# Hybrid block on one core: first modulations as plain fp32 on four column groups, filter steps in the opening stage

## The chip, the core and the metric

The kernel runs on one core of a Trainium2 chip. A core has TensorE (PE, the matmul array, with its weight loads listed apart as PEld), VectorE (DVE), ScalarE (ACT), GpSimd (POOL) and SyncE (SP). Each engine takes its instructions strictly in the order in which the built program lists them, and waits on semaphores where one needs another's result. Weights come from device memory by DMAs that SP issues; POOL and ACT issue some smaller ones. The metric is the device time of one execution in microseconds (us); lower is better.

## What is computed

One layer of a diffusion block over 256 latent tokens `x` and 256 context tokens `ctx`, width 2048. Only the start concerns the change:

```
mod   = silu(c)     @ w_ada + b_ada        # 6 x 2048 numbers for x
mod_c = silu(c_ctx) @ w_ada[:, :4096] + b_ada[:4096]   # shift and scale for ctx
u     = x   * (1 + scale)   + shift        # first two parts of mod
u_ctx = ctx * (1 + scale_c) + shift_c
parts = u @ w_in                            # keys, values, gates, Hyena, ...

# Hyena filters: independent of x, from three small weight matrices
hid = sin(sin(feats @ w1 + b1) @ w2 + b2)
h   = (hid @ w3) * window                   # 256 x (2 orders, 2 directions, 1024)
kf  = fft(h_fwd, h_bwd)                     # spectra, used later by the long convolutions
```

So the first 4096 columns of `w_ada` (2048 x 4096 in fp32, 33.5 MB) must be read and multiplied by two vectors before any projection of `u` can start.

## The kernel before

**Splitting.** The large products run in a reduced type called fp32r. To keep fp32 accuracy each operand is split into a high and a low part: `split` (line 136) copies the high part on ACT (line 138) and subtracts it on DVE (line 139), and a product becomes three: high by high, high by low, low by high (`cm_block`, line 215, lines 220, 221, 223).

**First modulations.** The loop at line 381 goes over four quarters `q` of 512 columns, and over `part` (0 shift, 1 scale). For each it reads 2048 x 512 of `w_ada` in four DMAs of 1 MB into a page `raw` (`load4`, line 319), splits half a page at a time (`split_ring`, line 324: high part to `ring`, low part to a `wlo` buffer), and accumulates 32 products of 512 columns into the bank `pmod` (lines 396 and 397). Their stationary operand `csw` (line 205) has 128 columns: high of c, high of c_ctx, low of c, low of c_ctx, repeated 32 times; only four rows of `pmod` are used. `mod_columns` (line 369) turns the four rows into columns with four small products by `sel` (line 374).

**Beside it.** A list `later` holds steps of the quarter before: `mod_columns`, four `modulated` (line 357: transpose 128 columns of x and ctx, scale and shift on ACT, split), two `keys` (line 346: 48 products each of 256 columns into four banks) and one `gates_in` (line 337: 24 such products). One is taken after every second half page. Two calls of `next(filt)` run the two small sine layers of the Hyena filters (`filters`, line 241) here.

**The filter steps.** The eight large steps of `filters` (line 271 on: for four groups of 256 channels by two orders) each load a window and two slices of `w3` (POOL's DMAs), make four plain fp32 products (line 281), multiply by the window, add and subtract the two directions (lines 282, 289, 290), split (line 292), and take 30 fp32r products of 256 columns with the Fourier matrix (`dft_mm`, lines 237 to 239). They use three pages each. Before, they are emitted in pairs after each of the four blocks of the DeltaNet's value projection (lines 685 to 698), where 192 products of 256 columns stand ready on PE per block.

**Order and buffers.** A scheduler orders each engine's list from the program's order and a timeline of its own. There are seven pages of 8 KB per partition (`k8`); in this stage they hold x and ctx (`xt`), `raw`, `csw`, and in filter steps `dfts`, `win`, `smdf`, `shl`. Accumulators of this stage come from four banks called `ps`, of which `gates_in` keeps one.

Of the kernel before, what the change touches and what calls it, by code (L numbers as in the profile page):

```python
# [16 lines left out]
P = 128  # L17
# [63 lines left out]
def tile_block(ctx: ExitStack, tc: tile.TileContext, A: dict, out: bass.AP):  # L81
# [6 lines left out]
    # SBUF slots by size in KB per partition: projections' operands 16, one more 16, pages 8, small ones  # L88
# [20 lines left out]
    def page(name, *shapes, dt=F32):  # L109
        """One 8 KB slot, cut into tiles of the given free shapes."""  # L110
        return cut(slot([P, 2048], "k8", name, dt), shapes)
# [21 lines left out]
    def bc(ap, shape):  # L133
        return ap.to_broadcast(shape)

    def split(src, hi, lo):
        """src = hi + lo exactly, each of at most 12 significant bits"""
        copy(out=hi, in_=src)  # L138
        tt_(out=lo, in0=src, in1=hi.bitcast(F32), op=SUB)  # L139
# [9 lines left out]
    # work that goes on beside the projections: some steps of it with each tile of weights  # L149
# [42 lines left out]
    def as_rows(ap):  # L192
# [9 lines left out]
    # stationary for one k-tile: columns hi of c, hi of c_ctx, lo of c, lo of c_ctx, over and over  # L202
    cs4 = slot([P, KT, 4], "k1", "cs4", F32R)
    split(csil.rearrange("p a k -> p k a"), cs4[:, :, 0:2], cs4[:, :, 2:4])
    csw = page("csw", (KT, P), dt=F32R)
    nc.vector.tensor_copy(out=csw.rearrange("p k (r c) -> p k r c", c=4),
                          in_=bc(cs4.bitcast(F32).unsqueeze(2), [P, KT, 32, 4]))
    sel = cst.tile([4, 2], F32, name="sel")
    tt_(out=sel, in0=ident[0:4, 0:2], in1=ident[0:4, 2:4], op=ADD)
# [5 lines left out]
    def cm_block(ps, wh, wl, ch, k, acts, first, last):  # L215
        """channel-major: 128 columns of w stationary; acts: (column range of the bank, hi, lo) of 256 tokens"""
# [98 lines left out]
    ring = slot([P, 4, 1024], "m16", "ring", F32R)  # L315
    turn = [0]
    raws = {}

    def load4(ap, k0, c0):
        raw = page("raw", (4, 512))  # L320
        nc.sync.dma_start(out=raw, in_=ap[k0 * P:(k0 + 4) * P, c0:c0 + 512].rearrange("(k p) c -> p k c", p=P))
        return raw

    def split_ring(raw):
        """two k-tiles by 512 columns, in two parts, with more of them under way"""
        n = turn[0]
        turn[0] += 1
        hi = ring[:, n % 4].rearrange("p (k c) -> p k c", k=2)
        lo = slot([P, 2, 512], ("whi", "wlo")[n % 2], "wlo", F32R)
        split(raw, hi, lo)  # L330
        return hi, lo

    psk = [mm_ps() for _ in range(4)]      # projected keys of the DeltaNet, by 128 channels

    pga = sc_ps()                          # and the inputs of its gates

    def gates_in(k0):
        raw, wh, wl = [slot([P, 4, P], "wraw", "wg", t) for t in (F32, F32R, F32R)]
        nc.sync.dma_start(out=raw, in_=w_in[k0 * P:(k0 + 4) * P, C_AB:C_AB + P].rearrange("(k p) c -> p k c", p=P))
        split(raw, wh, wl)  # L340
# [5 lines left out]
    def keys(k0):  # L346
        if k0 % 4 == 0:
            raws["k"] = load4(w_in, k0, C_DK)
        wh, wl = split_ring(raws["k"][:, k0 % 4:k0 % 4 + 2, :])
# [19 lines left out]
    def mod_columns(mod, part, pmod, q):  # L369
        """four times 128 columns of one modulation, from rows"""  # L370
        row = slot([4, 512], "k2", "modrow")
        copy(out=row, in_=pmod[0:4, :])
# [7 lines left out]
    later = []  # L380
    for q in range(4):
# [6 lines left out]
        for part in range(2):  # L388
            pmod = sc_ps()
            for kb in range(8):  # L390
                if kb % 2 == 0:
                    raw = load4(w_ada, kb * 2, part * D + q * 512)
                wh, wl = split_ring(raw[:, (kb % 2) * 2:(kb % 2) * 2 + 2, :])
                for k in range(2):
                    kt = kb * 2 + k
                    mm(pmod, csw[:, kt, :], wh[:, k, :], start=(kt == 0), stop=False)
                    mm(pmod, csw[:, kt, :], wl[:, k, :], start=False, stop=(kt == KT - 1))
                if later and (part * 8 + kb) % 2 == 1:
                    later.pop(0)()
            later.insert(0, lambda mod=mod, part=part, pmod=pmod, q=q: mod_columns(mod, part, pmod, q))  # L400
# [5 lines left out]
        if q in (1, 2):  # L406
            later.append(lambda: next(filt))
# [3 lines left out]
    # the remaining small vectors  # L411
# [20 lines left out]
    # lower bounds: softmax over the layers (one), cumulated, less the first  # L432
# [14 lines left out]
    def proj_cm_ctx(col0):  # L447
        """256 columns of w_in, channel-major: two banks of 128 channels by x 256 | ctx 256"""
# [11 lines left out]
    def proj_cm(wap, col0, ah, al):  # L460
        """256 columns, channel-major: one bank of 128 channels by 2 chunks by x 256"""
# [10 lines left out]
    def tm_accum(pss, ah, al, wap, k0, nk, c0):  # L472
        """512 columns, token-major: pss[i] += a[tokens of tile i].T w, a in two parts by k-tile"""
# [1067 lines left out]
```

## Time and profile before

| | us |
|---|---|
| median of 3 runs | 2402.77 |
| lowest, highest | 2392.48, 2405.41 |
| profiled execution: span from first to last instruction | 2405.1 |
| opening stage (to the last key and gate product) | 0 to 164.6 |
| value and query projections of the DeltaNet, with the filter steps | 166.3 to 372 |
| TensorE busy over the span | 2303.7 (96%) |

The profiled execution's span of 2405.1 us stands beside 2405.41 us for the slowest of the three runs, so hardly anything lies around the span; the median of the runs is 2.3 us below it. TensorE's busy time counts modelled ends of pipelined matmuls, so the true pace of a matmul is read from the distance between two starts, not from its duration. The granted clock of TensorE has two levels, 2.4 GHz (1.00) and 1.2 GHz (0.50).

### The profile page before, as it was taken

The numbers are of one execution on the slowest core, as the hardware profiler recorded it, in microseconds if no ns is written. First come the engines' busy times: TensorE is split into PE (matmuls) and PEld (weight loads), VectorE is DVE, ScalarE is ACT, GpSimd is POOL, SyncE is SP. The second block draws the span as 40 slices with busy tenths as digits, with TensorE's granted clock in tenths as the row PEclk, the third lists the DMA queues.
The fourth block names the chain that finished last, engine by engine and source line by source line (L and its number), as shares of the span: only waits on it lengthen the run. The fifth ranks groups of instructions, "written<-read, shape, count | busy, mean of one in ns | idle before, by whom it ended". The sixth has DMA issues, their size and how long they took to land.

```text
span 2405.1 us, 37191 instructions
## 1 busy us (share of the span) xinstructions
PE 2303.7 (96%) x14769; PEld 2071.4 (86%) x14769; DVE 1620.5 (67%) x2135; ACT 1049.5 (44%) x1416; POOL 174.3 (7%) x290
## 2 busy tenths in 40 slices
PE   6999999999999999899999998998999999999998
PEld 4899999898999999887888877778978977988986
DVE  6764567877799898876566656776655655555557
ACT  6677344443343343535443533434434433443442
POOL 0002220000200000311100110000000000000000
PEclk9999999999999999999999999999999999999999
DMA  9946468787552332797777798784667767657664
GB/s 333 334 151 193 146 187 260 232 260 248 165 143 86 106 115 81 212 248 246 241 227 228 263 320 259 262 293 145 205 221 233 248 215 231 203 190 225 192 201 149
DMA packets 295851, 510.97 MB, mean 212 GB/s; under 512 B 17414, under 2 KB 155105, under 8 KB 293084
## 3 DMA queue, kind: packets, MB, share of 16 engines
q1 hardware_dynamic: 271488, 422.63, 55.5%
q0 software_dynamic: 21408, 81.48, 10.9%
q10 hardware_dynamic: 2780, 4.47, 0.5%
q8 instruction: 116, 1.90, 0.3%
q14 instruction: 59, 0.48, 0.1%
HBM read 474.07 MB, written 34.45 MB: 211 GB/s over the span
## 4 chain that ended last, share of the span: by engine, by line
PE 67%; DMA 17%; DVE 9%; issue 4%; ACT 2%; DVEq 0%; ACTq 0%; SPq 0%
DMA aw<-in_w_ada_dram 11%; PE mm L223 10%; PE mm L221 10%; PE mm L220 10%; DVE wlo L139 5%; PE mm L482 5%; PE mm L483 4%; PE mm L481 4%; PE mm L800 3%; PE mm L801 3%; PE mm L799 3%; DMA wraw<-in_w_in_dram 2%; DMA wraw<-in_w_branch_dram 2%; PE mm L934 1%; PE mm L935 1%
## 5 line engine op out<-in xcount | busy, mean ns | idle before, releaser
L138 ACT CAST whi<-wraw 128x1024 fp32r<-128x1024 f32 x584 | 612.3, 1050 | 980.6 <-PE mm L221 267.7
L139 DVE TENSOR_TENSOR wlo<-wraw,whi 128x1024 fp32r<-128x1024 f32 x584 | 707.8, 1221 | 302.4 <-PE mm L223 87.4
L517 DVE SCALAR_TENSOR_TENSOR acc<-aw,csil,acc 128x1024 f32<-128x1024 f32 x120 | 154.0, 1284 | 235.6 <-DMA aw<-in_w_ada_dram 235.2
L223 PE MATMUL mm<-uxh,wlo 128*128 128x256 f32 x1024 | 292.4, 286 | 2.7 <-DVE wlo L139 2.7
L223 PE MATMUL mm<-u2h,wlo 128*128 128x256 f32 x1024 | 290.1, 283 | 1.6 <-DVE wlo L139 1.6
L220 PE MATMUL mm<-u2h,whi 128*128 128x256 f32 x1024 | 289.8, 283 | 0.5 <-ACT u2h L138 0.5
L221 PE MATMUL mm<-u2l,whi 128*128 128x256 f32 x1024 | 289.8, 283 | 0.3 <-DVE u2l L139 0.3
L220 PE MATMUL mm<-uxh,whi 128*128 128x256 f32 x960 | 274.6, 286 | 1.7 <-DVE cy L497 1.7
L221 PE MATMUL mm<-uxl,whi 128*128 128x256 f32 x960 | 274.8, 286 | 0.0
L482 PE MATMUL mm<-wlo,h 128*128 128x512 f32 x480 | 188.5, 393 | 13.6 <-DVE wlo L139 13.5
L223 PEld LDWEIGHTS mm<-uxh,wlo 128*128 128x128 f32 x1024 | 198.1, 193 | 3.9 <-DVE wlo L139 3.1
L223 PEld LDWEIGHTS mm<-u2h,wlo 128*128 128x128 f32 x1024 | 196.5, 192 | 2.6 <-DVE wlo L139 2.6
L220 PEld LDWEIGHTS mm<-u2h,whi 128*128 128x128 f32 x1024 | 196.6, 192 | 1.1 <-ACT u2h L138 0.9
L221 PEld LDWEIGHTS mm<-u2l,whi 128*128 128x128 f32 x1024 | 196.5, 192 | 0.7 <-DVE u2l L139 0.5
L221 PEld LDWEIGHTS mm<-uxl,whi 128*128 128x128 f32 x960 | 185.8, 194 | 2.1 <-issue 2.0
L220 PEld LDWEIGHTS mm<-uxh,whi 128*128 128x128 f32 x960 | 185.9, 194 | 1.9 <-ACT cy L528 1.9
L483 PE MATMUL mm<-whi,h 128*128 128x512 f32 x480 | 187.4, 390 | 0.0
L481 PE MATMUL mm<-whi,h 128*128 128x512 f32 x480 | 186.7, 391 | 0.0
L800 PE MATMUL mm<-wlo,uxh 128*128 128x512 f32 x384 | 152.9, 398 | 6.4 <-DVE wlo L139 6.4
L801 PE MATMUL mm<-whi,uxl 128*128 128x512 f32 x384 | 152.1, 396 | 0.0
L799 PE MATMUL mm<-whi,uxh 128*128 128x512 f32 x384 | 150.8, 401 | 0.8 <-ACT whi L138 0.8
L223 PE MATMUL mm<-uch,wlo 128*128 128x256 f32 x448 | 127.6, 286 | 0.0
(540 smaller groups left out, 4685.7 us busy)
## 6 DMA issues: line engine op xcount, KB each, us to landing
wraw<-in_w_in_dram SPq DMA_DIRECT2D x264, 512.0 KB, 4.7
wraw<-in_w_ff_dram SPq DMA_DIRECT2D x256, 512.0 KB, 4.1
aw<-in_w_ada_dram SPq DMA_DIRECT2D x128, 512.0 KB, 4.9
raw<-in_w_ada_dram SPq DMA_DIRECT2D x32, 1024.0 KB, 7.0
wraw<-in_w_branch_dram SPq DMA_DIRECT2D x48, 512.0 KB, 6.2
wraw<-in_w_out_dram SPq DMA_DIRECT2D x32, 512.0 KB, 5.9
g_d<-gate POOLq DMA_DIRECT2D x24, 256.0 KB, 5.2
gatel<-g_d POOLq DMA_DIRECT2D x24, 256.0 KB, 6.7
```

Source lines behind the costliest of these rows:

```text
L138: copy(out=hi, in_=src)
L139: tt_(out=lo, in0=src, in1=hi.bitcast(F32), op=SUB)
L220: mm(ps[:, sl], wh[:, k, cs], ah, start=first and i == 0, stop=False, skip_group_check=True)
L221: mm(ps[:, sl], wh[:, k, cs], al, start=False, stop=False, skip_group_check=True)
L223: mm(ps[:, sl], wl[:, k, cs], ah, start=False, stop=last, skip_group_check=True)
L481: mm(pss[i], a, wh[:, k, :], start=(kt == 0), stop=False)
L482: mm(pss[i], a, wl[:, k, :], start=False, stop=False)
L483: mm(pss[i], b, wh[:, k, :], start=False, stop=(kt == nk - 1))
L517: stt(out=acc, in0=a, scalar=csil[:, 0, kt:kt + 1], in1=acc, op0=MUL, op1=ADD)
L799: mm(pg[i], a, wh[:, k, :], start=(kt == 0), stop=False)
L800: mm(pg[i], a, wl[:, k, :], start=False, stop=False)
L801: mm(pg[i], c, wh[:, k, :], start=False, stop=(kt == KT - 1))
```

## The change

The stationary operand of the first modulations becomes `cs32`, 32 columns per k-tile, of which the first two are c and c_ctx in plain fp32 and the others zero. The weights are not split. The four k-tiles of one loaded megabyte go to four groups of 32 array columns, each group writing its own 32 rows of `pmod`; `sel` then adds the four groups when `mod_columns` turns rows to columns (a copy of 128 rows instead of 4). A loaded megabyte goes alternately to one of two halves of `ring` and to a page. `keys` and `gates_in` use the ordinary `wload` (their `raw` is two DMAs of 512 KB instead of one of 1 MB). `mod_columns` of part 0 runs at once. All ten steps of `filt` are in `later`: four at the start, two after each of the first three quarters; the two calls per value block are gone, and the steps of `later` are spread over the remaining megabytes of a quarter.

```diff
-    cs4 = slot([P, KT, 4], "k1", "cs4", F32R)
-    split(csil.rearrange("p a k -> p k a"), cs4[:, :, 0:2], cs4[:, :, 2:4])
-    csw = page("csw", (KT, P), dt=F32R)
-    nc.vector.tensor_copy(out=csw.rearrange("p k (r c) -> p k r c", c=4),
-                          in_=bc(cs4.bitcast(F32).unsqueeze(2), [P, KT, 32, 4]))
-    sel = cst.tile([4, 2], F32, name="sel")
-    tt_(out=sel, in0=ident[0:4, 0:2], in1=ident[0:4, 2:4], op=ADD)
+    cs32 = slot([P, KT, 32], "k4", "cs32")
+    nc.vector.memset(cs32, 0.0)
+    nc.vector.tensor_copy(out=cs32[:, :, 0:2], in_=csil.rearrange("p a k -> p k a"))
+    sel = cst.tile([P, 2], F32, name="sel")
+    tt_(out=sel, in0=ident[:, 0:2], in1=ident[:, 32:34], op=ADD)
+    for j in (2, 3):
+        tt_(out=sel, in0=sel, in1=ident[:, 32 * j:32 * j + 2], op=ADD)
...
-    ring = slot([P, 4, 1024], "m16", "ring", F32R)
+    ring = slot([P, 2, 4, 512], "m16", "ring")
...
+    def load_ada(k0, c0):
+        n = turn[0]
+        turn[0] += 1
+        raw = ring[:, n // 2 % 2] if n % 2 == 0 else page("raw", (4, 512))
+        nc.sync.dma_start(out=raw, in_=w_ada[k0 * P:(k0 + 4) * P, c0:c0 + 512].rearrange("(k p) c -> p k c", p=P))
+        return raw
...
-        if k0 % 4 == 0:
-            raws["k"] = load4(w_in, k0, C_DK)
-        wh, wl = split_ring(raws["k"][:, k0 % 4:k0 % 4 + 2, :])
+        wh, wl = wload(w_in, k0, 2, C_DK, 512)
...
-        row = slot([4, 512], "k2", "modrow")
-        copy(out=row, in_=pmod[0:4, :])
+        row = slot([P, 512], "k2", "modrow")
+        copy(out=row, in_=pmod)
...
-    later = []
+    later = [lambda: next(filt) for _ in range(4)]
...
-            for kb in range(8):
-                if kb % 2 == 0:
-                    raw = load4(w_ada, kb * 2, part * D + q * 512)
-                wh, wl = split_ring(raw[:, (kb % 2) * 2:(kb % 2) * 2 + 2, :])
-                for k in range(2):
-                    kt = kb * 2 + k
-                    mm(pmod, csw[:, kt, :], wh[:, k, :], start=(kt == 0), stop=False)
-                    mm(pmod, csw[:, kt, :], wl[:, k, :], start=False, stop=(kt == KT - 1))
-                if later and (part * 8 + kb) % 2 == 1:
+            for kb in range(4):
+                raw = load_ada(4 * kb, part * D + q * 512)
+                for j in range(4):
+                    mm(pmod[32 * j:32 * j + 32, :], cs32[:, 4 * kb + j, :], raw[:, j, :],
+                       start=(kb == 0), stop=(kb == 3))
+                for _ in range(-(-len(later) // (8 - 4 * part - kb))):
                     later.pop(0)()
...
-        if q in (1, 2):
-            later.append(lambda: next(filt))
+        if q < 3:
+            later += [lambda: next(filt) for _ in range(2)]
...
-            next(filt)
-            next(filt)
```

The start of TensorE's list before: after the one transposition of the small vectors come only products of the first modulations, each pair behind a split (`ring` is the high part, `wlo` the low).

```order
L171 MATMUL ps_75<-idon,colA_rows_68 128x128 [waits DMAHW3_49,DMAHW4_49,DMAHW2_49,DMAHW5_49,DMAHW0_49,DVE_49]
L396 MATMUL ps_112<-ring_102,csw_83 128x512 [waits DVE_49,Activation_49]
L397 MATMUL ps_112<-wlo_115,csw_83 128x512 [waits DVE_49]
L396 MATMUL ps_112<-ring_102,csw_83 128x512
L397 MATMUL ps_112<-wlo_115,csw_83 128x512
L396 MATMUL ps_112<-ring_102,csw_83 128x512 [waits Activation_49]
L397 MATMUL ps_112<-wlo_122,csw_83 128x512 [waits DVE_49]
```

The same place in the change. `L385` are the first modulations, four to a megabyte; `L258` are the two sine layers, `L282` the window products of the first filter step (`L281` before) and `L238` its first Fourier product (`L237` before).

```order
L171 MATMUL ps_75<-idon,colA_rows_68 128x128 [waits DMAHW3_49,DMAHW5_49,DMAHW1_49,DMAHW7_49,DMAHW0_49,DVE_49]
L385 MATMUL ps_112<-ring_102,cs_3_80 32x512 [waits DVE_49]
L385 MATMUL ps_112<-ring_102,cs_3_80 32x512 x3
L258 MATMUL ps_127<-fT_118,w_18_120 64x256 [waits DMASW2_49,DMASW1_49]
L385 MATMUL ps_112<-raw_139,cs_3_80 32x512 [waits DMAHW4_49]
L385 MATMUL ps_112<-raw_139,cs_3_80 32x512 x3
L385 MATMUL ps_112<-ring_102,cs_3_80 32x512 [waits DMAHW2_49]
L385 MATMUL ps_112<-ring_102,cs_3_80 32x512 x3
L258 MATMUL ps_145<-z_129,w_19_122 64x256 [waits DMASW7_49,Activation_49]
L282 MATMUL ps_170<-win_167,z_147 128x256 [waits DMASW2_49,Activation_49]
```

The 256 products behind splits have become 128 behind a DMA alone, and the sine layers and the first filter step stand between them.

TensorE's list before at the end of a quarter (here the second), where products of the first modulations and of `gates_in` (`wg`) alternate:

```order
L374 MATMUL ps_362<-sel,modrow_571 128x2 [waits Activation_49]
L374 MATMUL ps_362<-sel,modrow_571 128x2 x3
L396 MATMUL ps_554<-ring_102,csw_83 128x512 [waits Activation_49]
L220 MATMUL ps_107<-uxh_98,wg_596 128x256 [waits PE_49]
L397 MATMUL ps_554<-wlo_581,csw_83 128x512 [waits DVE_49]
L396 MATMUL ps_554<-ring_102,csw_83 128x512
L397 MATMUL ps_554<-wlo_581,csw_83 128x512
```

The end of the second quarter in the change: the last two products of `gates_in`, one megabyte, and a filter step, whose Fourier products wait for DVE and ACT.

```order
L224 MATMUL ps_107<-uxh_98,wlo_540 128x256
L224 MATMUL ps_107<-uch_100,wlo_540 128x256
L385 MATMUL ps_471<-ring_102,cs_3_80 32x512 [waits DMAHW6_49]
L385 MATMUL ps_471<-ring_102,cs_3_80 32x512 x3
L282 MATMUL ps_575<-win_572,z_147 128x256 [waits DMASW5_49,PE_49]
L282 MATMUL ps_575<-win_572,z_147 128x256
L282 MATMUL ps_580<-win_572,z_147 128x256 [waits DMASW6_49,DVE_49]
L282 MATMUL ps_580<-win_572,z_147 128x256
L238 MATMUL ps_594<-shl_591,dfts_162 128x256 [waits Activation_49]
L238 MATMUL ps_608<-shl_591,dfts_162 128x256 [waits DVE_49]
L239 MATMUL ps_594<-shl_591,dfts_162 128x256 [waits DVE_49]
L240 MATMUL ps_594<-shl_591,dfts_162 128x256
```

Two whole filter steps now close each quarter, with one megabyte of first modulations inside the first of them and nothing else between the window products and the Fourier products.

TensorE's list before in the value projection (`vy` is a value chunk being transposed, `mm` the projection's banks), where a filter step's window products stand among the projection's:

```order
L220 MATMUL mm_2478<-uch_100,whi_2589 128x256
L171 MATMUL ps_2340<-idon,vy_2332 128x128 [waits PE_49,Activation_49]
L171 MATMUL ps_2340<-idon,vy_2332 128x128 x3
L281 MATMUL ps_2356<-win_2353,z_1273 128x256 [waits DMASW7_49,PE_49]
L281 MATMUL ps_2356<-win_2353,z_1273 128x256
L281 MATMUL ps_2361<-win_2353,z_1273 128x256 [waits DMASW0_49,PE_49]
L281 MATMUL ps_2361<-win_2353,z_1273 128x256
L221 MATMUL mm_2478<-ucl_101,whi_2589 128x256
L223 MATMUL mm_2478<-uxh_98,wlo_2590 128x256
```

The same kind of place in the change:

```order
L221 MATMUL mm_3030<-uxh_98,whi_3033 128x256
L171 MATMUL ps_3005<-idon,vy_2997 128x128 [waits Activation_49]
L171 MATMUL ps_3005<-idon,vy_2997 128x128 x3
L222 MATMUL mm_3030<-uxl_99,whi_3033 128x256
L221 MATMUL mm_3030<-uch_100,whi_3033 128x256
L222 MATMUL mm_3030<-ucl_101,whi_3033 128x256
```

The value projection is left with its own products and transpositions.

## Rows read from the trace of the kernel before

**Rows 1.** The page, part 1: busy time, share of span, instructions by engine.

```profile
PE 2303.7 (96%) x14769; PEld 2071.4 (86%) x14769; DVE 1620.5 (67%) x2135; ACT 1049.5 (44%) x1416; POOL 174.3 (7%) x290
```

**Rows 2.** Busy time by stretch: PE, PEld, DVE, ACT, POOL, PE clock, DMA share, GB/s.

```profile
0.00:164.60 164.60, 145.33 (x871) 122.55 (x871) 111.78 (x158) 111.56 (x163) 6.29 (x15) 0.98 0.81 283
...
0.00:20.00 20.00, 7.65 (x19) 5.05 (x19) 8.80 (x14) 10.23 (x12) 2.50 (x8) 0.99 0.90 309
...
60.00:100.00 40.00, 40.00 (x255) 35.25 (x254) 29.25 (x34) 28.71 (x42) 0.52 (x1) 1.00 0.96 335
...
166.30:372.00 205.70, 205.11 (x1630) 197.90 (x1631) 116.60 (x212) 105.20 (x203) 43.99 (x70) 1.00 0.59 179
```

**Rows 3.** PE's groups by line: busy us, mean ns, idle before; 0:164.6, then 235:375.

```profile
L397 PE MATMUL ps<-wlo,csw 128*128 128x512 f32 x128 | 55.6, 437 | 5.1 <-DVE wlo L139 5.1
L396 PE MATMUL ps<-ring,csw 128*128 128x512 f32 x128 | 53.9, 424 | 7.0 <-ACT ring L138 7.0
...
L281 PE MATMUL ps<-win,z 64*128 64x256 f32 x64 | 17.0, 396 | 0.0
```

**Rows 4.** PE in order of time: start us, us, line, op, shapes, idle before.

```profile
10.46 0.79 PE L396 MATMUL ps<-ring,csw 128*128 128x512 f32 x1 [3.42 <-ACT ring L138]
...
40.30 1.05 PE L374 MATMUL ps<-sel,modrow 4*128 4x2 f32 x8 [0.66 <-ACT modrow L372]
...
43.36 0.40 PE L396 MATMUL ps<-ring,csw 128*128 128x512 f32 x1
43.59 0.39 PE L397 MATMUL ps<-wlo,csw 128*128 128x512 f32 x1
...
148.56 1.47 PE L171 MATMUL ps<-idon,xt 128*128 128x128 f32 x12
...
166.32 0.35 PE L220 MATMUL mm<-uxh,whi 128*128 128x256 f32 x1 [1.68 <-DVE cy L497]
...
240.15 0.28 PE L220 MATMUL mm<-uxh,whi 128*128 128x256 f32 x1
240.27 0.28 PE L221 MATMUL mm<-uxl,whi 128*128 128x256 f32 x1
...
242.48 1.99 PE L281 MATMUL ps<-win,z 64*128 64x256 f32 x8
244.40 0.38 PE L221 MATMUL mm<-ucl,whi 128*128 128x256 f32 x1
```

**Rows 5.** DVE and ACT in one filter step, and part of a sine layer, by time.

```profile
291.37 0.67 DVE L282 TENSOR_TENSOR win<-ps,win 128x512 f32<-128x512 f32 x1
...
292.82 0.27 DVE L287 MEMSET win<- 1x256 f32 x1
...
293.30 0.67 DVE L289 TENSOR_TENSOR smdf<-win 128x512 f32<-128x512 f32 x1
...
293.89 0.67 DVE L290 TENSOR_TENSOR smdf<-win 128x512 f32<-128x512 f32 x1
...
295.29 1.03 ACT L138 CAST shl<-smdf 128x1024 fp32r<-128x1024 f32 x1
...
296.35 1.23 DVE L139 TENSOR_TENSOR shl<-smdf,shl 128x1024 fp32r<-128x1024 f32 x1 [0.65 <-ACT shl L138]
...
115.91 1.32 DVE L263 SCALAR_TENSOR_TENSOR z<-z,z 64x256 f32<-64x256 f32 x3
```

**Rows 6.** Clock after a wait, 33.5 to 39.6 us; columns as in rows 2.

```profile
33.50:36.50 3.00, 0.56 (x2) 0.19 (x1) 1.24 (x2) 1.99 (x2) 0.00 (x0) 1.00 1.05 388
36.50:39.60 3.10, 3.06 (x7) 1.95 (x7) 1.12 (x1) 0.00 (x0) 0.00 (x0) 0.56 1.05 386
```

**Rows 7.** The chain of waits, 0:420 (start us, us, what), then one DMA issue group.

```profile
42.26 1.93 ACT uf L365 x4
...
raw<-in_w_ada_dram SPq DMA_DIRECT2D x32, 1024.0 KB, 7.0
```

More of the change, by code (lines that the diff above doesn't have):

```diff
@@ L314, in tile_block @@
     x_in, c_in = A["x"][0], A["ctx"][0]
-    ring = slot([P, 4, 1024], "m16", "ring", F32R)
+    ring = slot([P, 2, 4, 512], "m16", "ring")
     turn = [0]
[L317 to L324, printed above, removed]
+    def load_ada(k0, c0):
         n = turn[0]
         turn[0] += 1
[L328 to L331, printed above, removed]
+        raw = ring[:, n // 2 % 2] if n % 2 == 0 else page("raw", (4, 512))
+        nc.sync.dma_start(out=raw, in_=w_ada[k0 * P:(k0 + 4) * P, c0:c0 + 512].rearrange("(k p) c -> p k c", p=P))
+        return raw
     psk = [mm_ps() for _ in range(4)]
@@ L337, in gates_in @@
     def gates_in(k0):
-        raw, wh, wl = [slot([P, 4, P], "wraw", "wg", t) for t in (F32, F32R, F32R)]
-        nc.sync.dma_start(out=raw, in_=w_in[k0 * P:(k0 + 4) * P, C_AB:C_AB + P].rearrange("(k p) c -> p k c", p=P))
-        split(raw, wh, wl)
+        wh, wl = wload(w_in, k0, 4, C_AB, P)
         for k in range(4):
@@ L389, in tile_block @@
             pmod = sc_ps()
-            for kb in range(8):
-                if kb % 2 == 0:
-                    raw = load4(w_ada, kb * 2, part * D + q * 512)
-                wh, wl = split_ring(raw[:, (kb % 2) * 2:(kb % 2) * 2 + 2, :])
-                for k in range(2):
-                    kt = kb * 2 + k
-                    mm(pmod, csw[:, kt, :], wh[:, k, :], start=(kt == 0), stop=False)
-                    mm(pmod, csw[:, kt, :], wl[:, k, :], start=False, stop=(kt == KT - 1))
-                if later and (part * 8 + kb) % 2 == 1:
+            for kb in range(4):
[4 more added lines that the diff above has]
+                for _ in range(-(-len(later) // (8 - 4 * part - kb))):
                     later.pop(0)()
-            later.insert(0, lambda mod=mod, part=part, pmod=pmod, q=q: mod_columns(mod, part, pmod, q))
+            if part == 0:
+                mod_columns(mod, part, pmod, q)
+        later.append(lambda mod=mod, pmod=pmod, q=q: mod_columns(mod, 1, pmod, q))
         for cc in range(4):
```

## The prediction

> **What bounds the kernel now.** I read the page's busy shares first: TensorE is busy 96% of the span, no other engine above 67% [rows 1]. So the question for every edit is what it adds to or takes from TensorE's list, and where TensorE stands still. The stretches tell the two stages apart [rows 2]. In the opening stage (0 to 164.6 us) PE is busy 145.3 us, so it idles 19.3 us, and 12.4 of these lie in the first 20 us. From 60 to 100 us it is busy all the time while the DMA engines are at 0.96: both limits meet there, but PE has no hole left. From 166.3 to 372 us, where the filter steps now lie, PE is busy 205.1 of 205.7 us: every filter step there costs PE just its own products. By line [rows 3], the splits that the change removes hold PE up for 5.1 + 7.0 = 12.1 us in all. That is the most that freeing DVE and ACT can give here; the 67 and 44% of rows 1 are beside the point.
>
> Paces come from distances between starts [rows 4], since the durations overlap: an fp32r product of 512 columns 43.59 - 43.36 = 0.23 us; one of 256 columns 0.12; a transposition 1.47 / 12 = 0.12; the four products of `mod_columns` 1.05. A plain fp32 product shows as two records: 64 records in rows 3 for 8 steps of 4 products. Eight records take 244.40 - 242.48 = 1.92 us, 0.24 each for 256 columns. From 256 to 512 columns an fp32r product grows by 0.11; a plain record of 256 columns lasts twice an fp32r product, so I let it grow by 0.22: 0.46 us, or 0.92 for a whole plain product of 512 columns.
>
> **The opening stage before, as a check of these paces.** First modulations 256 x 0.23 = 58.9; keys and gates 480 x 0.12 = 57.6; transpositions 64 x 0.12 = 7.7; `mod_columns` 8 x 1.05 = 8.4; sine layers 1: together 133.6. With 19.3 idle that is 152.9 of 164.6 us; the other 11.7 us are stretches at half clock and small gaps.
>
> **First modulations: 128 plain products, four to a megabyte.** Nothing in the trace of before runs on separate column groups, so I bound it from both sides. All four at once: one product's time, 0.92 us per megabyte, 32 x 0.92 = 29.4. One after the other: 3.68 per megabyte, 117.8. Between them: the two records of a product use the same 32 columns and cannot overlap, but the second record of one group can run beside the first of the next if starts stay in order. Then eight records take five slots, 5 x 0.46 = 2.3 us, 73.6 in all. I take this value, because the rows show a product as two records in sequence; both ends stay for the range. So against 58.9 us PE saves 29, or pays 15, or pays 59.
>
> A page speaks for the first end: the Trainium skill, TensorEngine Tiling (Array Packing), section Key Properties, says that different tiles can load weights and multiply in parallel. No run of this kernel so far has shown it; by that rule the stage would be 44 us shorter than in my sum, and this is the first rival below. The same section says that changing the tiling mode drains TensorE, which would speak against the change, since each megabyte stands between full-width products; no row here gives a price for it.
>
> **Filter steps: 44 us of PE moved, and the cover lost.** A step has 4 x 0.48 + 30 x 0.12 = 5.5 us on PE; eight make 44.2 us (0.48 is two records). They leave the value projection, which has no holes: 44.2 us are saved there, and nothing else is late in their place, since PE waits there for 0.6 us only [rows 2]. In the opening stage they cost 44.2 again, plus what PE waits inside a step. The order shows nothing between the window products and the Fourier products. Rows 5 give that chain: second window product 0.67, memset 0.27, sum to difference 0.59, difference 0.67, high part 1.03, low part 1.23: 4.46 us, of which three Fourier products on the high part fill 0.36; with hand-overs 4.5. Eight times 4.5 = 36 us. In before these waits exist too, but 192 ready products per value block hide them. Here the only company would be keys and gates of the quarter before, and these stand ahead of the steps in the list. Below, the wait goes to nothing only if PE would wait for a load at that very moment anyway.
>
> **Start, modulated inputs, clock.** The first product starts at 10.46 us now [rows 4]. In the change DVE splits two blocks of keys ahead of the copy that `cs32` needs, and ACT casts four: some 2 + 2 us more, so 14.5. Between the second sine layer and the first window products stand a chain of small DVE operations (1.32 for three of seven) and the sine [rows 5]: 3 us. Each quarter's first keys wait for four activations, 1.93 us [rows 7], which before lie beside splits and modulations: 4 x 1.9 = 7.6. After some 2.4 us of waiting (33.5 to 36.5 us) the granted clock is 0.56 over the next 3.1 us, that is mostly at the lower level [rows 6]: 3.1 x 0.44 = 1.4 us lost. Eight such waits and the start: 12.
>
> **Loads.** The 32 loads of a megabyte stay [rows 7]; the filter steps add 8 x 0.9 = 7 MB (0.25 window, 0.13 weights, 0.5 spectra) to some 43 (33.5 modulations, 4.2 x and ctx, 4.2 keys, 1 gates). At the 335 GB/s of rows 2 these 50 MB take 150 us, less than PE's sum below, with three to four megabytes in flight by the ring's halves and the pages. I put nothing down for them. SP's list has ring loads ahead of page loads that are needed sooner; the 10 us of a filter step cover a landing of 7.0. POOL's list has the filters' loads in front of nothing urgent.
>
> **The sum.** PE's work to the end of the opening stage: 57.6 + 7.7 + 8.4 + 1 + 44.2 = 118.9, with 73.6 it is 192.5. Waits: 14.5 + 3 + 36 + 7.6 + 12 = 73.1. The stage ends at 265.6 us instead of 164.6, 101.0 later, and 44.2 come back in the value projection: +56.8 us. On the profiled execution that gives 2405.1 + 56.8 = 2461.9; on the median of the runs, which lies 2.3 lower, 2460. Beyond 372 us I expect nothing.
>
> **Rivals.** *All four groups side by side* (29.4): the stage ends at 221.4, the change is +12.6, about 2415. For it: four groups on separate columns and rows of the bank need nothing of each other. Against: the two records per product. *No overlap, so the change does not do what it says* (117.8): +101.0, about 2504. For it: every pair of products in the trace follows in sequence; nothing shows otherwise. *Faster*: the groups run side by side and the steps' waits are hidden, because loads and not PE set the pace, as the DMA share of 0.96 in rows 2 suggests. Then 36 of waits and 12 of clock go: 12.6 - 48 = -35, about 2368. It decides when a megabyte's landing comes later than the end of a filter step, that is when a quarter's loads (12 MB, 36 us at 335 GB/s) take longer than its PE work (36 us with this price, 49 with waits and clock). The balance is against it, but not by much. *Splits as the real bound*: freeing DVE and ACT gives at most the 12.1 us above, and is inside this case.
>
> **How the numbers follow.** Middle case (2460) 0.40; side by side (2415) 0.26; no overlap (2504) 0.19; faster (2368) 0.15. The predicted time is the middle case's. Each case has some 20 us either way by its waits, which are sums of short rows. The range leaves out most of the fastest case and the upper part of no overlap: 2395 to 2512. Within 0.5% (12 us, about what a measurement of this kernel can tell from no change) falls half of side by side and a little of the faster case: 0.15. Faster by more: 0.12. Slower by more: 0.73. The middle case alone would span 2440 to 2480, all of it slower.
>
> **What would show it.** In the profile of the changed kernel: distances between the starts of the eight records of a megabyte (five slots of 0.46, or two, or eight); PE's idle time ahead of the Fourier products, with DVE and ACT as releasers, near 36 us in all; the stage's end, near 265 us; the value projection shorter by 44 us without new waits; the granted clock in the opening stage well below 0.98. I am wrong if PE waits there for DMAs instead of DVE and ACT, if the groups need two slots, or if the value projection does not give its 44 us back.

## The result, and the profile after

The changed kernel takes 2440.16 us (median of 4 runs, 2437.04 to 2441.78) against 2400.95 us of the kernel before on the same chip: ratio 1.0159, 95% interval 1.0135 to 1.0183. The forecast was 2460 in a range of 2395 to 2512, slower by over 0.5% with a chance of 0.73. Direction and range held: 39 us slower where 57 were forecast, so the size was some 20 us too high. Terms of the sum were far off in opposite directions.

The page of the changed kernel: busy time by engine, then the first of 40 slices of the span and the granted clock in tenths. They answer [rows 1].

```profile
PE 2297.0 (94%) x14769; PEld 2050.0 (84%) x14769; DVE 1550.2 (64%) x2073; ACT 990.7 (41%) x1351; POOL 174.0 (7%) x290
...
PE   4788999999999999899999999999999999999998
...
PEclk8888999999999999999999999999999999999999
```

The same row of the page before:

```profile
PE   6999999999999999899999998998999999999998
```

What is new lies in the first four slices, some 244 us. There PE is busy four, seven, eight and eight tenths of the time (before: six, then nine), at a clock of 0.8. By stretch (PE, PEld, DVE, ACT, POOL, clock, DMA share, GB/s), as in [rows 2]:

```profile
60.00:100.00 40.00, 33.94 (x252) 22.80 (x252) 6.80 (x16) 11.11 (x23) 5.36 (x9) 0.87 0.81 274
...
0.00:250.69 250.69, 184.38 (x1176) 140.64 (x1176) 79.26 (x164) 73.47 (x133) 35.55 (x64) 0.85 0.66 220
250.69:412.00 161.31, 161.31 (x1357) 161.14 (x1358) 80.54 (x149) 87.73 (x174) 19.00 (x27) 1.00 0.60 186
```

The opening stage now ends at 250.69 us, where the next stage's first product stands (before: 166.32 in [rows 4]), 84.4 us later. In it PE idles 250.69 - 184.38 = 66.3 us, against 19.3 before (21.0 up to 166.32), and the mean clock is 0.85. The DMA share has fallen from 0.81 to 0.66, and only 5.4 us of waits for loads of weights are left in it (below): the loads no longer set the pace. The value projection behind it has no hole at all, and it gives much back: from the last product of the gates' inputs to the first Fourier product of the Hyena operator it is 211.4 us (249.77 to 461.14) where before it was 258.0 (164.36 to 422.33). So 85.4 us are lost, 46.6 given back, 38.8 remain at that mark and 35.0 at the end of the profiled span.

What ended PE's waits in the opening stage (us in total, times, longest):

```profile
PE ps L238 <- ACT shl L138: 30.4, 8, 5.2
PE ps L171 <- DMA colA_rows<-in_b_ada_dram: 12.7, 1, 12.7
PE ps L385 <- DVE cs L205: 9.4, 1, 9.4
PE ps L385 <- DMA ring<-in_w_ada_dram: 5.4, 1, 5.4
PE ps L239 <- DVE shl L139: 2.7, 8, 0.5
```

L238 and L239 are the Fourier products of a filter step: eight waits, 33.1 us. The two rows with `colA_rows` and `cs` are the start: 22.1 us until the modulations' stationary operand exists. What stands ahead of it on ACT and DVE (the activation `csil` needs the copy `colA`, and `cs32` needs `csil`):

```profile
17.91 1.22 DVE L139 TENSOR_TENSOR wlo<-wraw,whi 128x1024 fp32r<-128x1024 f32 x1 [1.50 <-ACT whi L138]
19.05 0.28 DVE L189 COPY colA<-ps 128x128 f32<-128x128 f32 x1
19.65 1.04 ACT L138 CAST whi<-wraw 128x1024 fp32r<-128x1024 f32 x1 [0.77 <-DMA wraw<-in_w_in_dram]
22.01 0.23 ACT L201 ACTIVATE csil<-colA 128x32 f32<-128x32 f32 x1
```

One filter step in order of time (start us, us, line, op, idle before), then the clock of its pieces:

```profile
150.82 1.99 PE L282 MATMUL ps<-win,z 64*128 64x256 f32 x8
156.56 0.79 PE L238 MATMUL ps<-shl,dfts 128*128 128x256 f32 x2 [3.75 <-ACT shl L138]
157.82 0.58 PE L239 MATMUL ps<-shl,dfts 128*128 128x256 f32 x1 [0.46 <-DVE shl L139]
```
```profile
150.82:156.56 5.74, 1.99 (x12) 1.42 (x8) 3.29 (x7) 1.04 (x1) 0.00 (x0) 0.93 0.88 304
156.56:162.73 6.17, 5.70 (x24) 5.27 (x25) 1.21 (x1) 0.59 (x1) 0.00 (x0) 0.51 0.41 149
162.73:165.00 2.27, 2.27 (x17) 1.27 (x17) 0.27 (x1) 1.43 (x3) 0.90 (x2) 1.00 0.00 0
```

PE stands still for 3.75 us behind the window products, and the Fourier products that follow run at a granted clock of 0.51, that is at 1.2 instead of 2.4 GHz, for 6.2 us; then it is back at 1.00. So the wait is paid a second time, in the products behind it.

The column groups themselves do well. First two of four megabytes back to back, then one between full-width products:

```profile
60.87 1.06 PE L385 MATMUL ps<-ring,cs 128*32 128x512 f32 x8
61.75 1.04 PE L385 MATMUL ps<-raw,cs 128*32 128x512 f32 x8
...
145.92 0.28 PE L224 MATMUL mm<-uch,wlo 128*128 128x256 f32 x1
146.12 1.07 PE L385 MATMUL ps<-raw,cs 128*32 128x512 f32 x8
147.12 0.38 PE L222 MATMUL ps<-ucl,whi 128*128 128x256 f32 x1
147.34 0.28 PE L224 MATMUL ps<-uxh,wlo 128*128 128x256 f32 x1
```

From start to start a megabyte, four products and eight records, takes 0.86 us. Between full-width products there is a little more: 0.20 instead of 0.12 ahead of it, 1.00 until the next one, and 0.22 instead of 0.12 for that one, 0.32 us in all.

### The profile page after: what moved, and what is told of

Its sections match the earlier page's. It is cut to its first block, busy times and chain, and to the rows that moved or that the text cites. A ratio compares the mean times of both kernels' runs of the same rounds, so it can differ in the third digit from the quotient of the medians.

```text
span 2440.1 us, 37035 instructions
## 1 busy us (share of the span) xinstructions
PE 2297.0 (94%) x14769; PEld 2050.0 (84%) x14769; DVE 1550.2 (64%) x2073; ACT 990.7 (41%) x1351; POOL 174.0 (7%) x290
## 4 chain that ended last, share of the span: by engine, by line
PE 65%; DMA 17%; DVE 11%; issue 5%; ACT 2%; POOL 0%; DVEq 0%; SPq 0%; ACTq 0%; POOLq 0%
DMA aw<-in_w_ada_dram 12%; PE mm L224 9%; PE mm L221 9%; PE mm L222 9%; DVE wlo L139 5%; PE mm L473 5%; PE mm L474 5%; PE mm L472 4%; PE mm L789 3%; PE mm L790 3%; PE mm L788 3%; DMA wraw<-in_w_branch_dram 2%; PE ps L385 1%; DMA wraw<-in_w_in_dram 1%; DVE acc L508 1%
## 5 line engine op out<-in xcount | busy, mean ns | idle before, releaser
L138 ACT CAST whi<-wraw 128x1024 fp32r<-128x1024 f32 x596 | 623.3, 1047 | 1010.3 <-PE mm L222 287.8
L139 DVE TENSOR_TENSOR wlo<-wraw,whi 128x1024 fp32r<-128x1024 f32 x596 | 720.5, 1217 | 369.1 <-PE mm L224 103.4
L221 PE MATMUL mm<-uxh,whi 128*128 128x256 f32 x1024 | 290.3, 286 | 0.6 <-DVE cy L488 0.6
L222 PE MATMUL mm<-uxl,whi 128*128 128x256 f32 x1024 | 290.3, 285 | 0.0
L221 PEld LDWEIGHTS mm<-uxh,whi 128*128 128x128 f32 x1024 | 196.4, 193 | 4.2 <-ACT whi L138 1.7
L222 PEld LDWEIGHTS mm<-uxl,whi 128*128 128x128 f32 x1024 | 197.1, 193 | 0.0
```

What stands on the lines that cost most here:

```text
L221: mm(ps[:, sl], wh[:, k, cs], ah, start=first and i == 0, stop=False, skip_group_check=True)
L222: mm(ps[:, sl], wh[:, k, cs], al, start=False, stop=False, skip_group_check=True)
```

## The experiments

**Theory**: the column groups run side by side and cost 0.9 us per megabyte; the loss is the filter steps in a stage where nothing covers their waits, those waits a second time through the clock, and a later start. **Rival A**: the groups, or the switch between narrow and full-width products, cost the time. **Rival B**: loads and buffers pace the stage, so waits of PE cost little. **Rival C**, for the clock alone: it is low for another reason than the waits. "Stage end" below is the start of the last product of the gates' inputs (before 164.4, after 249.8). The ratio of each run is to the kernel before, which gave 2400.3 to 2402.3 us beside these runs. The rest of the kernel varies by some 5 us either way from one execution to the next, so small differences are read at the stage end, in the one profiled execution of each run.

### One half alone: the column groups

The changed kernel with the filter steps back where they were (edit to the changed kernel; `next(filt)` twice per value block again):

```
-    later = [lambda: next(filt) for _ in range(4)]
+    later = []
...
-        if q < 3:
-            later += [lambda: next(filt) for _ in range(2)]
+        if q in (1, 2):
+            later.append(lambda: next(filt))
```

> Only one half of the change: first modulations in plain fp32 on four column groups, the filter steps where they were before (two sine layers in quarters 1 and 2, eight steps in the value projection). Theory (the groups run side by side, 0.9 us per megabyte; the loss of the whole change is waits in and around the filter steps): TensorE saves 58.9 - 29 = 30 us of the opening stage and the value projection stays at 206 us; with a first product as late as in the changed kernel (12 us later than before) the stage ends near 147 us instead of 164.6, and the kernel takes 2385 us; with the start as before 2372. Rival A (the groups cost more than their records show, for instance at each change between narrow and full-width products): 2401 or more. Rival B (loads and buffers pace the opening stage): the stage ends no earlier than some 155 us, 2390 to 2400, with TensorE waiting for DMAs.

Measured: 2395.09 us (8 runs), ratio 0.9987 (0.9967 to 1.0007); stage end 162.6. This is in rival B's range; the theory had 2385. By its time alone rival A (2401 or more) would not be excluded. It falls by the trace: up to the stage end PE is busy 117.9 us, where [rows 2] have 145.3, so the groups do save 27 of the 30 us that they were to save. But almost nothing of it arrives; the stage ends 1.7 us sooner. Three stretches of this kernel, and its waits:

```profile
0.00:162.63 162.63, 117.89 (x870) 82.55 (x871) 39.68 (x99) 51.06 (x99) 6.31 (x15) 0.94 0.83 290
20.00:40.00 20.00, 6.57 (x40) 2.20 (x40) 0.78 (x3) 3.14 (x4) 0.00 (x0) 0.87 1.06 382
40.00:60.00 20.00, 11.42 (x68) 3.87 (x68) 1.16 (x5) 4.45 (x11) 0.00 (x0) 0.79 1.05 387
```
```profile
PE ps L385 <- DMA ring<-in_w_ada_dram: 17.6, 5, 10.1
PE ps L171 <- DMA colA_rows<-in_b_ada_dram: 11.9, 1, 11.9
PE ps L385 <- DVE cs L205: 11.6, 1, 11.6
```

The DMA engines are full from 20 to 60 us, and PE waits 17.6 us for ring loads and 23.5 us for the start (first product at 23.95 us). Rival B holds for this half: without the filter steps in it, the first part of the opening stage is paced by its loads, and faster products there wait longer.

### The other half alone: the filter steps

The kernel before, with split parts, and all filter steps in the opening stage:

```
-    later = []
+    later = [lambda: next(filt) for _ in range(4)]
...
-                if later and (part * 8 + kb) % 2 == 1:
-                    later.pop(0)()
+                if (part * 8 + kb) % 2 == 1:
+                    for _ in range(-(-len(later) // (8 - (part * 8 + kb) // 2))):
+                        later.pop(0)()
...
-        if q in (1, 2):
-            later.append(lambda: next(filt))
+        if q < 3:
+            later += [lambda: next(filt) for _ in range(2)]
...
-            next(filt)
-            next(filt)
```

> Only the other half: all ten filter steps in the opening stage (four in the first quarter, two in each of the next three), the first modulations in split parts on full-width products as before. Theory: each of the eight steps leaves TensorE waiting 3.8 to 4.2 us for ACT and DVE and another 2.5 us at the lower clock, 8 x 6.4 = 51 us, less what split products that stand between take up: 2401 + 35 to 51 = 2436 to 2452. Rival A (the groups are the loss): near 2401. Rival B (loads pace the stage, so waits are hidden behind landings): 2401 to 2415.

Measured: 2487.49 us, ratio 1.0360 (1.0330 to 1.0390); stage end 284.3. That is more than the theory gave, by some 40 us. A part of it are waits that the theory did not have:

```profile
PE ps L237 <- ACT shl L138: 24.6, 8, 3.8
PE ps L396 <- ACT ring L138: 8.9, 5, 3.3
PE ps L396 <- ACT smdf L297: 7.1, 2, 4.0
PE ps L397 <- DVE wlo L139: 5.3, 8, 0.9
```

The steps' own waits are there (with L238, 28.1 us), and beside them 21 us ahead of the modulations' products (L396, L397), which wait for their split parts or for a bank. ACT's list shows one such place (start us, us, what, idle before):

```profile
136.02 1.99 ACT L138 CAST ring<-raw 128x1024 fp32r<-128x1024 f32 x2 [6.44 <-DMA raw<-in_w_ada_dram]
137.92 1.06 ACT L297 COPY smdf<-ps 128x512 f32<-128x512 f32 x2
```

The casts of a megabyte that has not landed stand ahead of the copies that take a filter's spectrum out of its bank; PE's next product waited 3.09 us for those. With unsplit weights there is no cast in ACT's list to stand in the way, and the changed kernel does not have these 21 us of waits. But it starts its first product 12 us later (22.51 against 10.50 here) and waits 5.4 us for a load. Up to the stage end, this run and then the changed kernel:

```profile
0.00:284.25 284.25, 217.81 (x1174) 178.89 (x1174) 150.46 (x213) 130.20 (x191) 34.43 (x62) 0.89 0.57 190
0.00:249.77 249.77, 184.09 (x1175) 140.53 (x1175) 78.34 (x162) 72.61 (x132) 35.55 (x64) 0.85 0.67 220
```

PE idles 66.4 us in the one and 65.7 in the other, so the 34.5 us between the two stage ends are PE's own busy time (217.8 against 184.1), above all the cheaper modulations (58.9 us before, 27.5 on the groups, at full pace). The rest is lost between the stage end and the Hyena operator (224.0 us here, 211.4 in the changed kernel).

So the two halves are not a sum: alone they give -5 (not clear of noise) and +87 us, together +39. With the filter steps in the stage the groups are worth 47 us, since there PE sets the pace and its saved time arrives; without them, 5, since there it ends in waits for loads and in the later start.

### The same 32 columns four times

```
-                    mm(pmod[32 * j:32 * j + 32, :], cs32[:, 4 * kb + j, :], raw[:, j, :],
-                       start=(kb == 0), stop=(kb == 3))
+                    mm(pmod[0:32, :], cs32[:, 4 * kb + j, :], raw[:, j, :],
+                       start=(kb == 0 and j == 0), stop=(kb == 3 and j == 3))
```

(`mod_columns` then takes 32 rows of `pmod` and of `sel` instead of 128.)

> The changed kernel with the four products of a megabyte on the same 32 columns, one after the other, instead of on four groups. Theory (groups run fully side by side): a megabyte takes 4 x 0.86 = 3.4 us instead of 0.86, 32 x 2.6 = 83 us more on TensorE, none of it inside a wait of a filter step: about 2520. If groups shared time (five slots, as the prediction took): 32 x 1.4 = 45 us more, 2485. Rival A (the switch of column groups is the cost): less than 40 us more.

Measured: 2509.4 us, ratio 1.0449 (1.0420 to 1.0478), 69 us more than with four groups. One megabyte, warm:

```profile
108.00 3.62 PE L385 MATMUL ps<-ring,cs 128*32 128x512 f32 x8
```

Four products in sequence take 3.62 us as modelled (1.04 with four groups). The difference, 2.6 us times 32, is the expected 83 us; 14 of them are taken up: up to the stage end (317.5) PE idles 58.5 us instead of 65.7, the load wait of 5.4 us being gone, and it is busy at half clock for 41.5 us instead of 55.2, which is worth 7. Five slots would have given 45, so this bears out full overlap.

### Keys between the halves of a filter step

```
                 split(smdf, h_, l_)
+                yield
...
-    later = [lambda: next(filt) for _ in range(4)]
+    later = [lambda: next(filt) for _ in range(6)]
...
         for kb in range(2):
+            if q < 3:
+                later.append(lambda: next(filt))
             later.append(lambda k0=4 * q + 2 * kb: keys(k0))
+            if q < 3:
+                later.append(lambda: next(filt))
...
-        if q < 3:
-            later += [lambda: next(filt) for _ in range(2)]
```

> The changed kernel with each filter step cut in two behind its split, and the products of half of a quarter's keys listed between the two halves. By the order of the instructions three of the eight steps then have 52 or more key products between window products and Fourier products; the other five are as before. Theory: three waits of 3.8 us and the lower clock behind them (2.5 us) go, 3 x 6.3 = 19 us: 2421. Rival B (loads and buffers pace the stage): the three waits come back as waits for DMAs, 2435 to 2440. Rival A: 2435 to 2440.

Measured: 2426.92 us, ratio 1.0108 (1.0088 to 1.0129), 13 us less than the changed kernel (19 were expected); stage end 235.9 instead of 249.8.

```profile
PE ps L238 <- ACT shl L138: 26.8, 5, 7.4
```

Eight waits have become five. Their sum fell by only 3.6 us, because some uncovered steps now wait longer (in the one at 106 us, 6.7 us: DVE waited 3.23 us there for the step's row of `hy_skip` to land), but the Fourier products of the covered steps run at full pace. Rival B predicted that the waits would come back as waits for DMAs; 5.5 us are there, where 5.4 were before. It falls for the changed kernel.

### Filling the waits with work

```
                     ps = sc_ps()
+                    for _ in range(36 if i2 == 0 else 0):
+                        mm(ps[:, 0:256], dh[:, 0, 0:P], dh[:, 1, 0:256], start=True, stop=True)
```

> The changed kernel with 36 products more in each filter step, between window products and Fourier products: a constant by a constant, into the bank that the first Fourier product overwrites, so that the result is the same and TensorE computes 36 x 0.12 = 4.3 us while it would wait 3.8. 288 products are added in all, 34.6 us of work. Theory (the waits cost twice, once as idle time and once more by the lower clock behind them, 30 Fourier products at 0.21 instead of 0.12 us): the added work lies in the 33 us of waits, the granted clock stays up, and 8 x 2.5 = 20 us go: 2420. Rival C (the clock is low for another reason, for instance the narrow or plain fp32 products, or because loads are late): 2440 to 2455.

Measured: 2432.46 us, ratio 1.0128 (1.0113 to 1.0143); stage end 235.7. With 288 products more, the stage ends 14 us sooner. The last stretches of the changed kernel and then of this run, the lines of the filter steps in the same order, and last the sum over all stretches of the opening stage in which the granted clock was 0.50 (first number: their length; then PE's busy time in them):

```profile
126.30:180.10 53.80, 44.14 (x297) 34.78 (x300) 16.10 (x31) 15.22 (x30) 7.16 (x12) 0.84 0.72 237
180.10:233.00 52.90, 44.62 (x303) 35.09 (x303) 16.94 (x33) 15.48 (x30) 7.86 (x14) 0.87 0.47 153
...
126.30:180.00 53.70, 53.23 (x414) 43.38 (x407) 18.31 (x37) 20.94 (x45) 7.68 (x13) 1.00 0.83 275
180.00:233.00 53.00, 51.34 (x399) 45.29 (x398) 20.46 (x46) 18.35 (x35) 7.00 (x12) 1.00 0.43 125
```
```profile
L238 PE MATMUL ps<-shl,dfts 128*128 128x256 f32 x80 | 30.5, 414 | 30.4 <-ACT shl L138 30.4
...
L297 PE MATMUL ps<-dfts 128*128 128x256 f32 x288 | 37.8, 292 | 0.0
L238 PE MATMUL ps<-shl,dfts 128*128 128x256 f32 x80 | 20.9, 288 | 0.0
```
```profile
sum 75.09, PE 55.25 PEld 46.83 DVE 18.00 ACT 13.40 POOL 2.31; mean PE 6.14 PEld 5.20 DVE 2.00 ACT 1.49 POOL 0.26
...
sum 13.64, PE 9.69 PEld 6.49 DVE 3.36 ACT 0.63 POOL 2.32; mean PE 4.84 PEld 3.25 DVE 1.68 ACT 0.32 POOL 1.16
```

The clock is 1.00 where the changed kernel has 0.84 and 0.87, and the record of a Fourier product on the high part (L238) lasts 288 ns instead of 414. Nothing else was changed, so the low clock in the filter steps follows from PE standing still ahead of them, and rival C falls. (By the time alone it would not: 2432 lies between the two forecasts.) The two stretches at half clock that are left begin at 34.0 and 68.1 us, behind the wait for the second sine layer (3.3 us) and in the one long wait for a load (6.2 us). Of the 14 us 5.4 are lost again between the stage end and the Hyena operator, 3.9 of them in waits for `hyc` there (9.0 us instead of 5.1).

### The start

```
+    for tag in ("wraw", "wraw", "wraw", "wraw", "whi", "whi", "whi", "whi"):
+        hold = slot([P, 2, 512], tag, "hold")
+        nc.vector.tensor_copy(out=hold[:, 0, 0:2], in_=csil[:, 0, 0:2])
     cs32 = slot([P, KT, 32], "k4", "cs32")
```

> The changed kernel with the buffers of the first key weights held until the first activation of the small vectors is done, by eight tiny copies on DVE, so that neither the loads nor the casts of key weights stand ahead of the column block that the first modulations need. Theory: in the changed kernel the first product comes at 22.5 us only because of these; it comes at 13 to 16 us then, and as TensorE and its waits, not the loads, set the pace of this stage, the kernel gains 7 us: 2433. Rival B (the loads pace the stage): the gain is eaten by a later wait for a load, 2438 to 2445.

Measured: 2433.3 us, ratio 1.0138 (1.0122 to 1.0155). That is the number that the theory had, but the interval overlaps the changed kernel's (1.0135 to 1.0183), so the stage end has to bear the reading.

```profile
11.43 1.94 PE L388 MATMUL ps<-ring,cs 128*32 128x512 f32 x8 [1.42 <-DVE cs L208]
```

The first product comes 11 us sooner and the stage ends 9.4 us sooner (240.4); the kernel's medians differ by 7. The late start of the changed kernel is thus the key weights' work in front of a short chain: on ACT four casts that wait for landings, on DVE two splits. For 3 of the 11 us it is `colA_rows`, which PE awaits for 9.6 instead of 12.7 us when the key weights' loads are held back.

### Looking for a better mixture

Column groups with two of the eight steps in the first quarter and six in the value projection (`later` begins with four steps; the value blocks take 2, 2, 1, 1):

> Column groups as in the run with that half alone, the two sine layers and two of the eight filter steps in the first quarter, as the changed kernel has them, the other six in the value projection. In the run with the groups alone TensorE stood 45 us in the first 62 us, with the DMA engines at 0.91 to 1.06. Theory (that stage is paced by loads, so TensorE has room for a filter step and its wait there): two steps leave the value projection, 2 x 5.5 = 11 us, and cost nothing ahead of it: 2395 - 11 = 2384. Against it: the steps' pages take buffers from the loads, and each step still has its 6 us of waiting and low clock: 2395 to 2402.

Column groups with three steps, one in each of the first three quarters, cut in two around the keys:

> Column groups, the two sine layers in the first quarter, and three of the eight filter steps in the opening stage, one with each of the first three quarters' keys and each cut in two behind its split with key products listed between; the other five in the value projection. By the order of the instructions 50 to 80 key products stand between window and Fourier products of each. Theory: a step whose wait is covered costs its own 5.5 us of products only, and of these the waits for loads take up a part: 2395 - 3 x 5.5 = 2379 if all of it, 2395 if none. If a covered step still costs more than an uncovered place in the value projection (buffers, loads), 2400 or more.

Measured: 2403.31 us, ratio 1.0008 (0.9996 to 1.0021), and 2403.52 us, ratio 1.0009 (0.9997 to 1.0021). Both expectations of a gain fell. Two uncovered steps move the stage end from 162.6 to 179.6 us, 8.5 each, and return 7.1 us behind it instead of 11. Three covered ones move it to 173.8, 3.7 each, less than their 5.5 us of products, but return 6.5 us instead of 16.5. Against those missing 10 us stand 8.6 us of waits behind the stage end:

```profile
PE ps L572 <- ACT gT L569: 4.3, 1, 4.3
PE mm L224 <- DVE wlo L139: 2.6, 1, 2.6
PE ps L171 <- DVE hyc L488: 1.7, 2, 1.2
```

With the groups alone there is 0.5 us of waiting there. So a covered step, too, gained nothing in this place over the value projection; that none could is not shown. The profiled execution is the fastest of this run's ten (2396.91 us), so its waits may be at the short end.

Column groups alone, with the start of the experiment above:

> Column groups alone (filters where they were before) with the buffers of the first key weights held until the first activation of the small vectors, as in the run of the start. Theory: with the groups alone the opening stage is paced by loads up to some 120 us (DMA engines at 0.91 to 1.06), so an earlier first product only lengthens later waits for loads: 2390 to 2396, no measurable difference to the 2395 without it. Rival D (what counts is when the first quarter's keys can start, since TensorE is busy without a hole from 62 us on and only 18 of the 62 us before are work): the holes ahead of 62 us shrink by the 7 to 9 us that the first product comes earlier, 2386 to 2388.

Column groups alone, the same eight buffers held until the first part of the first quarter's modulations is done (the copies read `mod` and stand behind the first `mod_columns`):

> Column groups alone, with the buffers of the first key weights held until the first part of the first quarter's modulations is done, so that the first eleven loads on SyncE's queue all belong to the first quarter's modulations (instead of seven, with four blocks of key weights between). Theory (loads pace the stage, whatever their order): 2390 to 2396. Rival D (the first quarter's keys start sooner, by the time of the 3.4 MB that are put behind, 10 us at the 380 GB/s of this stretch, on top of the earlier first product): 2378 to 2386.

Measured: 2397.23 us, ratio 0.9982 (0.9970 to 0.9994), and 2391.49 us, ratio 0.9960 (0.9944 to 0.9975). The first has no gain beyond the groups alone: the product that comes sooner waits for loads instead (30.9 us in six waits, where it was 17.6), and the stage ends at 164.3 us. Where loads set the pace, an earlier start was worth nothing; the same hold brought the stage end 9.4 us forward in the changed kernel, where they don't. The second changes which loads come first. It is faster than both kernels of this case, by 0.4% over before, with its stage end at 161.2 us in the profiled execution, the slowest of its six; the 10 us and more that rival D gave for it did not come, and the time lies in the theory's 2390 to 2396.

## Why the prediction was right, and where its steps were off

- **First modulations, the mis-sized term.** The step "eight records take five slots, 73.6" failed. The groups overlap fully: 32 x 0.86 = 27.5 us, 46 less. The bound of 0.92 per megabyte from [rows 4] was the right row; I gave more weight to the two records of a product than they carry. By the prediction's own list this was a sign of being wrong ("if the groups need two slots"): 0.86 us is two slots of 0.43 and not five. The Trainium skill, TensorEngine Tiling (Array Packing), section Key Properties, says that tiles multiply in parallel, and the trace agrees (0.86 us for four, 3.62 as modelled for four in one group). The same section of the Trainium skill says that a change of the tiling mode drains TensorE. What the trace shows there, whatever its cause, is 0.32 us around a megabyte between full-width products, 32 x 0.32 = 10 us at most, and it is no reason against the change.
- **Filter steps' waits.** 36 forecast, 33.1 measured, with the chain of [rows 5]. Right in place, releaser and size.
- **Clock, the second mis-sized term.** I took 1.4 us lost per wait from [rows 6], 12 in all. In the opening stage the granted clock was 0.50 for 75.1 us together, and PE was busy in 55.3 of them (the sum under *Filling the waits with work*); half of that, 27.6 us, is what the clock cost. Behind the one wait shown above it is 0.49 x 6.2 = 3.0 us. [rows 6] ends after 3.1 us, where the products that it shows end; a filter step goes on with 30. It was a lower bound, and I used it as the value.
- **Small gaps, put at nothing.** PE's work at full pace is 118.9 + 27.5 = 146.4 us, the idle time 66.3, the clock 27.6; of 250.7 us 10.4 are left, for small gaps and the products around a megabyte. The prediction's check of the kernel before left 11.7 us in the same way, "stretches at half clock and small gaps". In that trace the half clock cost 3.0 us (PE busy for 6.0 us at 0.50), so 8.7 of them were such gaps, and the sum did not carry them over.
- **Start.** 14.5 forecast, 22.5 measured, the time of the first product: the four casts on ACT are not 2 us of work but wait for landings, one after the other, and the last rows of `colA_rows`, too, came later: PE waited for them for 12.7 us, where it was 6.6 before.
- **Modulated inputs, loads.** 7.6 us for the activations showed up as 0.6 us of waiting; loads, put at nothing, cost 5.4 at one place. These nearly balance.
- **The sum.** -46 for the modulations, +16 for the clock, +10 for the small gaps, +5 for the idle time (66.3 against 61.1): -15, and the stage ends at 250.7 instead of 265.6. The value projection gave 46.6 us back where 44.2 was forecast, and no new wait stands in it; just ahead of the Hyena operator PE waits 5.1 us for `hyc`, where before it was 3.0 for `hv` and `hyc`. That the total came close is thus partly luck: with the clock alone sized rightly I would have forecast some 2476, and rightly sized groups with 12 us of clock would have given 2414, the rival *side by side*.
- **Rivals.** *Side by side* was the right mechanism for the groups, with too little for the clock and nothing for the small gaps. *Faster* needed loads to pace the stage. They did so in the kernel with the groups alone, as the DMA share in [rows 2] hinted, but not in the changed one, whose filter steps slowed PE below the loads. *Splits as the real bound*: the 12.1 us held for the kernel before; with the filter steps in between, the same products waited 21 us.

## What to carry to other kernels

A step with a serial chain across engines belongs where ready products of another chain stand beside it in PE's list; moved to a place without them, it costs its waits and then the half clock behind each wait, here 33 us of waits and some 25 us more by the clock (27.6 against 3.0 before). Before speeding up an engine's products in a stage, read the DMA share there: in a stage whose first 60 us were full of loads, 27 us of saved PE time moved the stage end by 1.7. Two edits that share engines are not a sum: here -5 and +87 made +39, because PE's saved time was lost to loads and a later start in the one setting and arrived in the other, where PE set the pace.

## What was not expected of the hardware

Plain fp32 products of 512 columns on four groups of 32 columns take 0.86 us for all four, about as long as one takes by itself (3.62 / 4 = 0.9): the two records of a product do not keep other groups from running. And adding 34.6 us of products made a stage end 14 us sooner, since PE no longer stood still in the filter steps and was then busy at 1.2 GHz for only 9.7 us instead of 55.3.
